# Mix loads, mix splits and first output weights of a streaming encoder step, moved among the sample pairs

## The chip, the cores and the metric

The kernel runs on one core of one Trainium2 chip. The metric is the device time of one execution in microseconds (us); lower is better. The engines are named as in the profile: PE (TensorE, matrix multiply; PEld is its weight load), DVE (VectorE), ACT (ScalarE), POOL (GpSimd) and SP (SyncE, which issues most of the DMA transfers, in program order).

## The reference

One layer of a streaming encoder, for a prompt of 1024 rows and a sample of 64 rows with caches. Cut to what matters here:

```python
h = rms_norm(xp, g_norm1[l])
qa, ka, va, qb, kb, vb, logf = in_proj(h, w_in[l], ...)
oa = chunk_band_attn_prompt(qa, ka, va, rel_bias[l])
ob = forget_attn_prompt(qb, kb, vb, logf)
xp = xp + jnp.concatenate([oa, ob], axis=-1) @ w_o[l]
mk, mv = mem_kv(mem_prompt, g_mem[l], w_mkv[l], g_mk[l])
...
oa = chunk_band_attn_sample(qa, ka, va, cache_a_k[l], cache_a_v[l], rel_bias[l])
ob = forget_attn_sample(qb, kb, vb, logf, cache_b_k[l], cache_b_v[l], cache_b_logf[l])
xs = xs + jnp.concatenate([oa, ob], axis=-1) @ w_o[l]
```

`concatenate([oa, ob])` is what the kernel calls the mix; the product with `w_o` is the output projection. The model width is 1024, the two attentions have 8 heads of 64 each, and the memory has 256 rows.

## The kernel before

Everything is computed in float32, each factor of a matmul split into a rounded high part and the rest as a low part: a product is three matmuls (high times high, low times high, high times low). A split is one cast on ACT (hi) and one subtraction on DVE or POOL (lo).

The stretch around the change lies between the prompt's attention, which ends at about 600 us, and the output projection, which begins at about 710 us. Three pieces of work share it.

**The memory's keys and values** (mem_piece, L679) are a list of pieces, `line`. Their weights come as loads `mwraw` of 512 KB (L661), two buffers, and are split in quarters, `mwhi` on ACT (L668) and `mwlo` on POOL or DVE (L669).

**The samples** are eight head pairs, one after the other (class Sample). For a pair, load fetches the query and key rows (`sqd`), the caches (`kraw`, `vraw`) and a bias; prep transposes and normalizes the query (`tq`, `sq`, `skn`); splitk and splitv split the caches (`kchi`, `kclo`, `vc`); score makes the scores `S` (L797, L798) and the exponential (L808); turn transposes the probabilities (`PT`, L822) and splits them (`pth` L823, `ptl` L824); sum multiplies them with the values into `O` (L835) and puts the halves together (`st` L842, `su` L843); out transposes `su` (L847) and copies it into `smix` (L849).

A loop over x = 0 to 8 weaves the steps of pair x, the rest of pair x - 1 and the preparation of pair x + 1 with `PER[x]` pieces of `line`. PER is (4, 8, 9, 12, 6, 5, 6, 0, 0), so at x = 7 `line` is empty.

**The prompt's mix** was written by the attention to a DRAM tensor `mixd`, eight tiles of 128 rows x 1024 columns. At x = 7, open_left closes the memory's buffers and, in their place, opens those of the weights (`wr`), of the first residual row (`x0`), of the split mix (`a`) and of four raw mixes (`mraw`). It loads the mixes (L976) and returns eight steps; each splits one tile over all 1024 columns, cast on ACT (L979) and subtraction on DVE (L980), and loads the mix four tiles on. The steps are woven in at x = 7. At x = 8 the first four weight tiles of `w_o` are split (class Stream: load L911, `hi` L919, `lo` L920) and the first product is woven in. After the loop the sample's columns are added to the split mix (L1022, L1023).

**The output projection** (project) goes over 8 tiles of output rows m and 3 chunks of columns c: 384, 384 and 320, the last with the sample's 64. A product of 24 matmuls (L937) fills a bank; DVE adds the residual row `qhi`, loaded by SP (L1066), in the evacuation (L1073), SP stores the result (L1074), and ACT, DVE and POOL make the operand and the square sum of the next norm (L1076 to L1083). ORDER starts with (m, c) = (0, 0), (0, 1), and these two products are the ones made early.

What stands in the code is not yet the order on the engines: a scheduler places the instructions of each engine.

Of the kernel before, what the change touches and what calls it, by code (L numbers as in the profile page):

```python
# [7 lines left out]
F32 = mybir.dt.float32  # L8
F32R = mybir.dt.float32r
ACT = mybir.ActivationFunctionType  # L10
ALU = mybir.AluOpType
# [4 lines left out]
P = 128  # L16
T = 1024
S = 64
N = T + S
D = 1024  # L20
KT = 8
# [6 lines left out]
PER = (4, 8, 9, 12, 6, 5, 6, 0, 0)  # L28
STAGE, MIXES = 4, 8
WARM = 20  # L30
# [4 lines left out]
CHUNKS = ((0, 384), (384, 384), (768, 320))  # L35
# [6 lines left out]
def hybrid_step(ctx: ExitStack, tc: tile.TileContext, i: dict, o: dict):  # L42
    nc = tc.nc
    act, dve, pool, pe = nc.scalar, nc.vector, nc.gpsimd, nc.tensor

    def f32(ap):
        return ap.bitcast(F32)
# [17 lines left out]
    mixd = dram.tile([8, P, T], F32, name="mixd")  # L65
# [38 lines left out]
    left = ExitStack()  # L104
# [355 lines left out]
    mixes = {}  # L460
# [183 lines left out]

    left = ExitStack()
    mp = left.enter_context(tc.tile_pool(name="mp", bufs=1, side="left"))
# [68 lines left out]
    class Sample:  # L715
# [180 lines left out]
    late_left, mixes = ExitStack(), ExitStack()  # L896
    stream = None

# [3 lines left out]
    class Stream:  # L902
# [52 lines left out]
    mixr = []  # L955
    first = [Product(2 * m, mixr, c, c == 2) for m, c in ((0, 0), (0, 1))]

# [4 lines left out]
    def open_left():  # L962
        nonlocal stream
        left.close()
        stream = Stream(late_left.enter_context(tc.tile_pool(name="wr", bufs=1, side="left")))
        x = late_left.enter_context(tc.tile_pool(name="x0", bufs=1, side="left")).tile([P, 384], F32, name="x0")
        nc.sync.dma_start(x, i["xT"][0, :, 0:384])
        ha = mixes.enter_context(tc.tile_pool(name="ha", bufs=1, side="left"))
        stage = rest.enter_context(tc.tile_pool(name="stage", bufs=1, side="left"))
        mixr.extend(parts(ha, "a"))  # L970
        stream.fetch()
        raws = {}

        def load_mix(k):
            raws[k] = stage.tile([P, T], F32, name="mraw", bufs=STAGE)
            nc.sync.dma_start(raws[k], mixd[k])  # L976

        def split_mix(k):
            act.copy(mixr[0][k][:, 0:T], raws[k])  # L979
            dve.tensor_tensor(mixr[1][k][:, 0:T], raws[k], f32(mixr[0][k][:, 0:T]), op=ALU.subtract)  # L980

        for k in range(STAGE):
            load_mix(k)

        def split_load(k):
            split_mix(k)
            if k + STAGE < KT:
                load_mix(k + STAGE)

        return ha, [lambda k=k: split_load(k) for k in range(KT)], x  # L990

    old, mixes_todo, ha = [], [], None
    todo = first[:]
    for x in range(len(samples) + 1):
        if not line and ha is None:
            ha, mixes_todo, early_x = open_left()
# [89 lines left out]

    ORDER = [(0, 0), (0, 1), (1, 0), (0, 2), (1, 1), (1, 2)] + [(m, c) for m in range(2, 8) for c in range(3)]

# [805 lines left out]
```

## Time and profile before

| | |
|---|---|
| median of 3 runs | 1781.4 us (1781.03 to 1784.44) |
| profiled execution | 1788.58 us, span 1786.6 us, granted clock 0.988 |
| busy share of the span | PE 96%, PEld 93%, DVE 68%, ACT 53%, POOL 36% |
| DMA | 199.87 MB, mean 112 GB/s |
| loads of a mix | 8 of 512 KB, median 5.0 us to landing |
| loads of memory weights | 16 of 512 KB, median 6.1 us to landing |

How to read the lines below. A row of the timeline has the start in us, the duration in us, the engine, the line in the kernel, the operation, output and inputs, shapes and a count; in brackets the idle time of the engine just before it, and what ended it. A row of the windows has a stretch, its length, and the busy time of each engine in it with the count of its instructions, then the granted clock of PE (1.00 is full speed), the busy share of the DMA engines and GB/s. A row of a line's instructions has the line, the engine, the operation and count, and the least, median and greatest duration in ns.

### The profile page before, as it was taken

Reading aid. Unit: us, or ns where it says so; the run is one execution under the profiler, and the core shown is the slowest. Engines: PE = TensorE matmul, PEld = TensorE weight load, DVE = VectorE, ACT = ScalarE, POOL = GpSimd, SP = SyncE. Lnnn points to the kernel's source line nnn. Section 1 sums busy time; section 2 is a strip of 40 time slices with the busy share of each in tenths; the row PEclk is TensorE's granted clock in tenths of the full one; section 3 lists DMA queues with packets and bytes.
Section 4 is the critical chain, followed back from the end, with each engine's and each line's share of the span. In section 5 each row is a group of like instructions: output and inputs, shape, how many; then the busy total and the mean of one; then the engine's idle time right before and its main releaser. Section 6 shows DMA issues by size and latency. Waiting matters only on the chain.

```text
span 1786.6 us, 33930 instructions
## 1 busy us (share of the span) xinstructions
PE 1717.5 (96%) x12432; PEld 1668.3 (93%) x12432; DVE 1210.5 (68%) x2643; ACT 941.2 (53%) x2058; POOL 647.3 (36%) x931
## 2 busy tenths in 40 slices
PE   7898999999998898999999999999999999999999
PEld 6888999999997777999999999999999999999999
DVE  5768667677677686433444369877777777649986
ACT  6756667677677577433555456434333333434432
POOL 4556667778777443453443612100000000000000
PEclk8999999999999999999999999999999999999999
DMA  7322222122112777541111563222222222693332
GB/s 251 91 62 64 60 77 78 49 74 76 51 56 83 216 252 219 165 143 56 54 54 60 151 214 104 79 75 77 79 85 85 85 73 73 216 346 130 118 104 88
DMA packets 134391, 199.87 MB, mean 112 GB/s; under 512 B 20984, under 2 KB 74360, under 8 KB 134224
## 3 DMA queue, kind: packets, MB, share of 16 engines
q1 hardware_dynamic: 134224, 197.70, 35.0%
q8 instruction: 98, 1.61, 0.4%
q14 instruction: 69, 0.57, 0.1%
HBM read 155.35 MB, written 45.44 MB: 112 GB/s over the span
## 4 chain that ended last, share of the span: by engine, by line
PE 46%; DVE 4%; issue 2%; ACT 1%; POOL 1%; DMA 1%; SPq 0%; DVEq 0%; ACTq 0%; POOLq 0%
PE W L1449 24%; PE W L1773 11%; PE pj L937 7%; PE S L1192 1%; PE tq L1228 1%; PE O L1228 1%; POOL lo L920 1%; DVE f L1314 0%; PE PT L1215 0%; DMA f<-x2d 0%; DVE lo L920 0%; DMA h<-ad 0%; PE O L1192 0%; ACT hi L1313 0%; DVE qhi L1301 0%
## 5 line engine op out<-in xcount | busy, mean ns | idle before, releaser
L299 PE MATMUL pj<-whi,xhi 128*128 128x384 f32 (+1 forms) x512 | 195.8, 382 | 2.7 <-DVE flog L314 1.6
L299 PE MATMUL pj<-wlo,xhi 128*128 128x384 f32 (+1 forms) x512 | 177.0, 346 | 4.3 <-POOL wlo L123 4.3
L299 PE MATMUL pj<-whi,xlo 128*128 128x384 f32 (+1 forms) x512 | 175.9, 344 | 0.7 <-DVE xlo L131 0.7
L1555 POOL COPY s<-gp 128x2 f32<-128x2 f32 x22 | 15.8, 720 | 335.8 <-DVE gp L1554 335.8
L1449 PE MATMUL W<-h,hi 128*128 128x272 f32 x704 | 134.4, 288 | 1.4 <-ACT qlo L1585 1.4
L504 ACT ACTIVATE s<-s,mx 128x640 f32<-128x640 f32 (+7 forms) x128 | 94.4, 737 | 77.4 <-DVE mx L502 76.5
L1773 PE MATMUL W<-f,hi 128*128 128x272 f32 x672 | 127.1, 287 | 0.1
L541 DVE TENSOR_TENSOR ptl<-PT,pth 128x512 fp32r<-128x512 f32 (+2 forms) x192 | 99.4, 522 | 37.5 <-ACT pth L540 35.3
L1449 PEld LDWEIGHTS W<-h,hi 128*128 128x128 f32 x704 | 110.8, 188 | 1.6 <-ACT qlo L1585 1.6
L540 ACT CAST pth<-PT 128x512 fp32r<-128x512 f32 (+2 forms) x192 | 84.7, 449 | 41.7 <-PE PT L539 39.9
L1773 PEld LDWEIGHTS W<-f,hi 128*128 128x128 f32 x672 | 105.3, 188 | 0.4 <-DVE f L1520 0.4
L299 PEld LDWEIGHTS pj<-wlo,xhi 128*128 128x128 f32 x512 | 99.5, 194 | 5.9 <-POOL wlo L123 5.9
L299 PEld LDWEIGHTS pj<-whi,xhi 128*128 128x128 f32 x512 | 99.4, 194 | 4.3 <-DVE flog L314 1.9
L1449 PE MATMUL W<-h,lo 128*128 128x272 f32 x352 | 101.8, 289 | 0.0
L299 PEld LDWEIGHTS pj<-whi,xlo 128*128 128x128 f32 x512 | 98.3, 192 | 1.4 <-DVE xlo L131 1.2
L1773 PE MATMUL W<-f,lo 128*128 128x272 f32 x336 | 96.7, 288 | 0.0
L539 PE MATMUL PT<-ident,s 128*128 128x128 f32 x528 | 89.9, 277 | 6.9 <-DVE ptl L541 5.4
L1313 ACT CAST hi<-raw 128x512 fp32r<-128x512 f32 x68 | 42.2, 621 | 98.6 <-PE W L1449 59.2
L499 PE MATMUL S<-kh,q 128*128 128x256 f32 (+1 forms) x304 | 77.8, 281 | 13.5 <-DVE mx L502 13.5
L937 PE MATMUL pj<-a,hi 128*128 128x384 f32 (+1 forms) x352 | 89.3, 337 | 0.2 <-DMA mraw<-mixd 0.2
L507 POOL TENSOR_SCALAR s<-s,ssum 128x640 f32<-128x640 f32 (+6 forms) x96 | 70.8, 738 | 47.9 <-DVE ssum L505 34.3
L554 PE MATMUL O<-pth,v 128*128 128x256 f32 (+1 forms) x304 | 76.5, 277 | 8.5 <-DVE mix L564 7.7
(538 smaller groups left out, 6037.6 us busy)
## 6 DMA issues: line engine op xcount, KB each, us to landing
raw<-in_w_down_dram SPq DMA_DIRECT2D x45, 256.0 KB, 2.8
wraw<-in_w_dram SPq DMA_DIRECT2D x56, 192.0 KB, 2.5
raw<-in_w_up_dram SPq DMA_DIRECT2D x41, 256.0 KB, 2.8
h<-ad SPq DMA_DIRECT2D x32, 272.0 KB, 5.5
mwraw<-in_w_mkv_dram SPq DMA_DIRECT2D x16, 512.0 KB, 6.1
raw<-in_w_mo_dram SPq DMA_DIRECT2D x32, 256.0 KB, 3.2
kvraw<-in_w_down_dram SPq DMA_DIRECT2D x32, 256.0 KB, 3.0
ad<-t SPq DMA_DIRECT2D x22, 272.0 KB, 2.2
```

The source lines that it names most:

```text
L299: pe.matmul(pj[:, :nw], x2[a][:, k, t * P:(t + 1) * P], wt[k][b][:, :nw], start=n == 0, stop=n == 3 * KT - 1)
L499: pe.matmul(sp[:, a:a + (k1 - k0) * P], q, kk[:, h, src], start=m == 0, stop=m == 1)
L504: act.activation(s[:, :n], s[:, :n], ACT.Exp, bias=mx, scale=-1.0, accum_out=sm)
L507: pool.tensor_scalar(s[:, :n], s[:, :n], sm, 1.0, op0=ALU.mult, op1=ALU.mult)
L539: pe.transpose(pt[:, b - ch[0]], self.s[j][:, (b - w0) * P:(b - w0 + 1) * P], ident)
L540: act.copy(hi[:, f:f + n, j], pt[:, f:f + n])
L541: dve.tensor_tensor(lo[:, f:f + n, j], pt[:, f:f + n], f32(hi[:, f:f + n, j]), op=ALU.subtract)
L554: pe.matmul(op[:, cols], groups[p, b // 2].v[:, b % 2, h].rearrange("p a d -> p (a d)"), pt[:, x, cols], start=b == self.full[0] and m == ...
L937: pe.matmul(out()[:, :cn], w[a][:, k % 4], x[b][k][:, c0:c0 + cn], start=k == 0 and n == 0, stop=k == KT - 1 and n == 2)
L1313: act.copy(hi, t)
L1449: pe.matmul(w[:, z, :Q], a(p, j), rights[j][b][:, z * Q:z * Q + Q], start=fresh and begin and j == 0 and x == 0, stop=final and end and j ...
L1773: pe.matmul(ws[m][:, z, :Q], la[p][:, m * P:(m + 1) * P], ra[b][:, z * Q:z * Q + Q], start=first and y == 0 and what in opening, stop=fina ...
```

## The change

The buffers of the weights and of the first residual row are opened before the memory's, so that they exist throughout. The mixes are loaded within the loop, at x = 4, 5 and 6 with two each and the last two in open_left, into five buffers of the samples' pool and three of the caches' `kraw` buffers. The query buffer `sqd` has one copy instead of two. Weights and residual row are fetched at x = 4, and the first four weight tiles are split at x = 5 and 6. The mix is split in two ranges of columns, 0 to 383 for all tiles and then 384 to 1023, sixteen steps instead of eight, eight of them at each x; the first product is woven with the second range. The second early product is (1, 0) instead of (0, 1), and ORDER follows.

```diff
-STAGE, MIXES = 4, 8
+MIXES = 8
+MIXED = {4: ("mraw",) * 2, 5: ("mraw",) * 2, 6: ("mraw", "kraw")}
+WEIGHTS = 5
...
-    left = ExitStack()
+    left, late_left = ExitStack(), ExitStack()
+    wr = late_left.enter_context(tc.tile_pool(name="wr", bufs=1, side="left"))
+    early_x = late_left.enter_context(tc.tile_pool(name="x0", bufs=1, side="left")).tile([P, 384], F32, name="x0")
     mp = left.enter_context(tc.tile_pool(name="mp", bufs=1, side="left"))
...
-            self.qd = mq.tile([S, 4, P], F32, name="sqd", bufs=2)
+            self.qd = mq.tile([S, 4, P], F32, name="sqd", bufs=1)
...
+    mraws = []
+
+    def load_mix(tag="mraw"):
+        k = len(mraws)
+        mraws.append(mq.tile([P, T], F32, name=tag, bufs={"mraw": 5, "kraw": 3}[tag]))
+        nc.sync.dma_start(mraws[k], mixd[k])
...
+    stream = Stream(wr)
...
-    first = [Product(2 * m, mixr, c, c == 2) for m, c in ((0, 0), (0, 1))]
+    first = [Product(2 * m, mixr, c, c == 2) for m, c in ((0, 0), (1, 0))]
...
     def open_left():
...
         left.close()
...
         mixr.extend(parts(ha, "a"))
...
-        def split_mix(k):
-            act.copy(mixr[0][k][:, 0:T], raws[k])
-            dve.tensor_tensor(mixr[1][k][:, 0:T], raws[k], f32(mixr[0][k][:, 0:T]), op=ALU.subtract)
...
-        return ha, [lambda k=k: split_load(k) for k in range(KT)], x
+        first_, rest_ = CHUNKS[0][1], slice(CHUNKS[0][1], T)
+
+        def split_mix(k, c):
+            hi, lo = (mixr[z][k][:, c] for z in range(2))
+            act.copy(hi, mraws[k][:, c])
+            dve.tensor_tensor(lo, mraws[k][:, c], f32(hi), op=ALU.subtract)
+
+        for k in range(6, KT):
+            load_mix("kraw")
+
+        return ha, [lambda k=k, c=c: split_mix(k, c) for c in (slice(0, first_), rest_) for k in range(KT)]
...
         if nxt:
             nxt.load()
+        for tag in MIXED.get(x, ()):
+            load_mix(tag)
+        if x == WEIGHTS - 1:
+            stream.fetch()
+            nc.sync.dma_start(early_x, i["xT"][0, :, 0:384])
...
-        if ha and not mixes_todo:
-            stream.upto(4)
-            if todo:
-                main = todo.pop(0).pieces
+        if WEIGHTS <= x < WEIGHTS + 2:
+            subs += [lambda n=n: stream.upto(n) for n in (2 * (x - WEIGHTS) + 1, 2 * (x - WEIGHTS) + 2)]
+        if ha and len(mixes_todo) <= KT:
+            main = todo.pop(0).pieces
         subs += mixes_todo[:MIXES]
...
-    ORDER = [(0, 0), (0, 1), (1, 0), (0, 2), (1, 1), (1, 2)] + [(m, c) for m in range(2, 8) for c in range(3)]
+    ORDER = [(0, 0), (1, 0), (0, 1), (0, 2), (1, 1), (1, 2)] + [(m, c) for m in range(2, 8) for c in range(3)]
```

Where this moves instructions shows in the order of the engines at three places. (Line numbers of the changed kernel are 2 to 12 higher.)

The first is ACT at the end of the prompt's attention, about 590 to 597 us in the profile before; `pth` are the casts of its probabilities, `s` its softmax. Before:

```order
L504 ACTIVATE s,ssum<-s,mx 128x896
L540 CAST pth<-PT 128x4x128
L540 CAST pth<-PT 128x3x128
L504 ACTIVATE s,ssum<-s,mx 128x1024
L509 ACTIVATE s<-s,ssum 128x896
L540 CAST pth<-PT 128x4x128 x2
L563 COPY otmp<-O 64x256
```

and with the change:

```order
L506 ACTIVATE s,ssum<-s,mx 128x896
L542 CAST pth<-PT 128x4x128
L929 CAST hi<-raw 128x512
L542 CAST pth<-PT 128x3x128
L506 ACTIVATE s,ssum<-s,mx 128x1024
L511 ACTIVATE s<-s,ssum 128x896
L542 CAST pth<-PT 128x4x128
L929 CAST hi<-raw 128x512
L542 CAST pth<-PT 128x4x128
L929 CAST hi<-raw 128x512
L565 COPY otmp<-O 64x256
```

Three casts of `w_o` weights (`hi<-raw`) have moved in between the last probability casts; in before, the first of them stands behind the last sample's transposes.

The second is SP at the loads of the last sample pair but one and of the last memory weights, about 676 us before:

```order
L740 DMA kraw<-in_cak_dram 128x512 x2
L744 DMA vraw<-in_cav_dram 128x512
L661 DMA mwraw<-in_w_mkv_dram 128x1024 x2
L702 DMA out_mv_dram<-kv 128x256
L703 DMA vmd<-kv 128x256
```

and with the change:

```order
L744 DMA kraw<-in_cak_dram 128x512 x2
L748 DMA vraw<-in_cav_dram 128x512
L902 DMA mraw<-mixd 128x1024 x2
L665 DMA mwraw<-in_w_mkv_dram 128x1024 x2
L706 DMA out_mv_dram<-kv 128x256
L707 DMA vmd<-kv 128x256
```

Two mixes now stand ahead of the two loads of memory weights.

The third is PE at the end of the samples, about 704 to 711 us before; `S` are the last pair's scores, `O` the weighted sums, `PT` the transposes of its probabilities, `pj<-a` the first product:

```order
L797 MATMUL S<-kclo,sq_9095 128x512
L835 MATMUL O<-vc,pth 128x256
L835 MATMUL O<-vc,ptl 128x256
L835 MATMUL O<-svh,pth 128x256
L835 MATMUL O<-svh,ptl 128x256
L847 MATMUL PT<-ident,su 64x128
L822 MATMUL PT<-ident,s 128x128 x4
L822 MATMUL PT<-ident,s 64x128
L937 MATMUL pj<-a_10467,hi 128x384
L937 MATMUL pj<-a_10475,hi 128x384
```

and with the change, at the start of the products:

```order
L839 MATMUL O<-vc,pth 128x256
L839 MATMUL O<-vc,ptl 128x256
L839 MATMUL O<-svh,pth 128x256
L839 MATMUL O<-svh,ptl 128x256
L949 MATMUL pj<-a_10506,hi 128x384 x2
L949 MATMUL pj<-a_10514,hi 128x384
L949 MATMUL pj<-a_10506,lo 128x384
L949 MATMUL pj<-a_10507,hi 128x384
```

Before, the first product starts behind the transposes of the last pair, and the last pair's sums stand within it; with the change all ten sums of the last pair stand ahead of the first product, and the two products (`x2` is one matmul of each) run side by side. In that order the query's transposes of the last pair (L758) and the sums of the pair ahead of it also stand behind the last memory matmul.

More of the change, by code (lines that the diff above doesn't have):

```diff
@@ L895, in hybrid_step @@
     step(0, [samples[0].prep, lambda: samples[0].splitk(0), lambda: samples[0].splitk(1)])
-    late_left, mixes = ExitStack(), ExitStack()
-    stream = None
+    mixes = ExitStack()
     srcs = [i[n][m][:, 4 * c:4 * c + 4] for n, ms in (("w_o", range(8)), ("w_mq", range(8)), ("w_mo", ROWS), ("w_mo", ROWS)) for m in ms for c in range(2)]
@@ L962, in open_left @@
     def open_left():
-        nonlocal stream
         left.close()
-        stream = Stream(late_left.enter_context(tc.tile_pool(name="wr", bufs=1, side="left")))
-        x = late_left.enter_context(tc.tile_pool(name="x0", bufs=1, side="left")).tile([P, 384], F32, name="x0")
-        nc.sync.dma_start(x, i["xT"][0, :, 0:384])
         ha = mixes.enter_context(tc.tile_pool(name="ha", bufs=1, side="left"))
-        stage = rest.enter_context(tc.tile_pool(name="stage", bufs=1, side="left"))
         mixr.extend(parts(ha, "a"))
[L971 to L976, printed above, removed]
-        def split_mix(k):
[L979 to L988, printed above, removed]
-        return ha, [lambda k=k: split_load(k) for k in range(KT)], x
+        first_, rest_ = CHUNKS[0][1], slice(CHUNKS[0][1], T)
[6 more added lines that the diff above has]
+        return ha, [lambda k=k, c=c: split_mix(k, c) for c in (slice(0, first_), rest_) for k in range(KT)]
     old, mixes_todo, ha = [], [], None
@@ L995, in hybrid_step @@
         if not line and ha is None:
-            ha, mixes_todo, early_x = open_left()
+            ha, mixes_todo = open_left()
         cur = samples[x] if x < len(samples) else None
```

## The prediction

> **What bounds the kernel now.** I read the page first, for the engine that is the bound.
>
> ```profile
> PE 1717.5 (96%) x12432; PEld 1668.3 (93%) x12432; DVE 1210.5 (68%) x2643; ACT 941.2 (53%) x2058; POOL 647.3 (36%) x931
> PE W L1449 24%; PE W L1773 11%; PE pj L937 7%; PE S L1192 1%; PE tq L1228 1%; PE O L1228 1%; POOL lo L920 1%; DVE f L1314 0%; PE PT L1215 0%; DMA f<-x2d 0%; DVE lo L920 0%; DMA h<-ad 0%; PE O L1192 0%; ACT hi L1313 0%; DVE qhi L1301 0%
> ```
>
> TensorE (PE) is busy 96% of the span and carries the chain of waits. The change leaves its matmuls as they are, so it can save only time in which PE idles, or in which it runs at a reduced clock. Next I cut the stretch of the change into windows.
>
> ```profile
> 680.00:700.00 20.00, 19.01 (x132) 16.18 (x131) 12.92 (x36) 13.84 (x36) 6.60 (x7) 1.00 0.67 211
> 700.00:710.00 10.00, 5.81 (x30) 4.18 (x30) 7.76 (x17) 8.90 (x20) 1.45 (x1) 0.85 0.75 232
> 710.00:725.00 15.00, 14.12 (x63) 12.62 (x63) 10.22 (x20) 9.07 (x23) 7.15 (x4) 0.76 0.53 174
> 725.00:740.00 15.00, 15.00 (x95) 15.00 (x94) 4.82 (x9) 6.07 (x12) 6.40 (x5) 1.00 0.68 206
> 760.00:806.00 46.00, 46.00 (x280) 46.00 (x279) 16.09 (x25) 16.76 (x32) 22.76 (x21) 1.00 0.45 144
> ```
>
> After each length come the busy times of PE, weight load, VectorE (DVE), ScalarE (ACT) and GpSimd (POOL), then granted clock, DMA share and GB/s. From 680 to 700 PE idles 1.0 us, from 700 to 710 4.2 us, from 725 on not at all. So the prize is what lies between 700 and 725: 5.1 us of idling (4.19 and 0.88) and a clock of 0.76 to 0.85. The timeline of that stretch says why.
>
> ```profile
> 703.68 0.40 PE L797 MATMUL S<-kclo,sq 128*128 128x512 f32 x1
> 705.05 0.78 ACT L808 ACTIVATE s<-s,mx 128x576 f32<-128x576 f32 x1 [0.95 <-DVE mx L807]
> 706.02 1.03 ACT L979 CAST a<-mraw 128x1024 fp32r<-128x1024 f32 x1
> 707.08 0.31 ACT L842 ACTIVATE st<-O,ssum 64x64 f32<-64x64 f32 x1
> 707.09 1.23 DVE L980 TENSOR_TENSOR a<-mraw,a 128x1024 fp32r<-128x1024 f32 x1 [0.48 <-ACT a L979]
> 708.34 0.29 DVE L843 SCALAR_TENSOR_TENSOR su<-O,ssum,st 64x64 f32<-64x64 f32 x1
> 708.78 0.39 PE L847 MATMUL PT<-ident,su 128*64 128x128 f32 x1 [4.03 <-DVE su L843]
> 709.02 1.31 PE L822 MATMUL PT<-ident,s 128*128 128x128 f32 x5
> 710.55 1.01 PE L937 MATMUL pj<-a,hi 128*128 128x384 f32 x2 [0.22 <-DMA mraw<-mixd]
> 724.76 0.51 PE L937 MATMUL PT<-a,hi 128*128 128x384 f32 x2
> ```
>
> The exponential of the last sample pair is done at about 706.0, yet PE stands still until 708.78: the two halves of su, which its next instruction reads, stand on ACT and DVE between whole 1024-wide splits of the mix (1.03 and 1.23 us). The first two products then run from 710.55 to 724.76. The last view is the granted clock, in windows of 3.41 us on the grid on which it changes in this trace.
>
> ```profile
> 17.57:20.99 3.42, 1.84 (x11) 1.52 (x10) 2.57 (x10) 3.42 (x12) 0.00 (x0) 1.00 0.93 277
> 92.67:96.08 3.41, 1.59 (x11) 1.30 (x11) 3.31 (x10) 1.31 (x4) 1.27 (x3) 1.00 0.24 53
> 703.65:707.06 3.41, 1.10 (x7) 0.72 (x5) 2.41 (x7) 2.45 (x5) 1.03 (x1) 1.00 0.82 255
> 707.06:710.48 3.42, 1.55 (x6) 0.97 (x6) 3.33 (x4) 3.32 (x7) 0.00 (x0) 0.50 0.88 271
> 713.89:717.30 3.41, 3.41 (x12) 3.41 (x12) 3.38 (x4) 2.72 (x10) 1.74 (x1) 0.50 0.88 326
> ```
>
> A window in which PE is busy 32% (703.65) is followed by half clock, and so is one of 47% (92.67); one of 54% (17.57) is not. The half clock lasts from 707.06 until after a full window, at 717.30. So in this trace about half a window of idling is enough to lose the clock.
>
> **The change, part by part.** The sum is made against the profiled execution, 1788.58 us (span 1786.6 us); the median of the runs is 1781.4 us, 7.18 us less, and the same difference is taken over to it.
>
> *Early weights.* Four splits of w_o weights go from behind 709 us into the end of the prompt's attention, three of them, by the order, before its last output.
>
> ```profile
> 590.00:606.00 16.00, 13.46 (x101) 11.93 (x101) 8.21 (x17) 8.88 (x19) 7.36 (x12) 1.00 0.70 189
> 596.64 0.38 PE L554 MATMUL O<-pth,v 128*128 128x256 f32 x1 [0.35 <-ACT pth L540]
> L919 ACT CAST hi<-raw x64: 602/620/635, 709.9 to 1073.0; 128x512 fp32r<-128x512 f32 x64
> L920 POOL TENSOR_TENSOR lo<-raw,hi x48: 1275/1293/2278, 710.6 to 1023.4; 128x512 fp32r<-128x512 f32 x48
> ```
>
> There PE waits for ACT's probability casts (0.35 us at 596.64), and the new casts of 0.62 us stand in front of such casts. If all three delay it: 3 x 0.62 = +1.9 us; if they fall into ACT's idle 45% (8.88 of 16 busy): 0. POOL is 46% busy there and takes its 1.29 us beside. I take +0.5, nearer the free end, since ACT is more often free than PE is waiting for it.
>
> *Mix loads beside the samples.* The mixes are 8 loads of 512 KB as before. Two of them now stand on the sync queue ahead of the last two loads of memory weights.
>
> ```profile
> 680.00:684.00 4.00, 4.00 (x30) 3.60 (x30) 2.79 (x7) 3.37 (x10) 1.66 (x2) 1.00 0.97 339
> 683.78 0.62 ACT L668 CAST mwhi<-mwraw 128x512 fp32r<-128x512 f32 x1 [0.43 <-DMA mwraw<-in_w_mkv_dram]
> 688.60 0.39 PE L679 MATMUL pj<-mwlo,mhi 128*128 128x256 f32 x1 [0.49 <-POOL mwlo L669]
> ```
>
> Here the DMA engines are full (0.97, 339 GB/s), and the weights arrive just in time: ACT waits 0.43 us for them at 683.78, PE 0.49 us for their split at 688.60. Two mixes ahead delay them by up to 2 x 524,288 bytes / 339 GB/s = 3.1 us. Behind them wait ACT's and POOL's splits, and PE behind those; its cover is the work of the sample pairs that the scheduler now places there. Between 0 and +3.1 I take +0.5, the row nearest to it, PE's present wait of 0.49, once more. That the query buffer has one copy instead of two costs at most one late small load, beside a full PE: 0.
>
> *The end of the samples.* The memory matmuls come earlier in PE's order, and behind the last of them stand only the two last sample pairs, one step after the other; both products come behind all of it. I walk this chain with durations of before.
>
> ```profile
> 698.44 0.40 PE L754 MATMUL tq<-ident,sqd 64*128 64x64 f32 x4
> 699.47 0.28 PE L679 MATMUL pj<-mwhi,mlo 128*128 128x256 f32 x1
> 700.31 0.87 PE L822 MATMUL PT<-ident,s 128*128 128x128 f32 x5
> 700.56 0.35 DVE L266 SCALAR_TENSOR_TENSOR skn<-tq,gd,skn 128x128 fp32r<-128x128 f32 x1 [0.63 <-ACT skn L265]
> 701.37 0.58 ACT L823 CAST pth<-PT 128x512 fp32r<-128x512 f32 x1
> 702.25 0.69 DVE L824 TENSOR_TENSOR ptl<-PT,pth 128x512 fp32r<-128x512 f32 x1
> 703.21 0.28 PE L835 MATMUL O<-vc,pth 128*128 128x256 f32 x1
> 703.33 0.28 PE L835 MATMUL O<-vc,ptl 128*128 128x256 f32 x1
> ```
>
> The last memory matmul ends at 699.75. To the end of the scores (704.08) it took 4.3 us, and 1.9 us more to the end of the exponential (705.05 + 0.97, with its accumulator read). Then come the transposes 0.87, the two halves of the probabilities 0.58 and 0.69, and ten sums at a step of 0.12 (703.21 to 703.33) = 1.2: together 9.6 us. But in before the query's transposes had been issued at 698.44, ahead of that end, and the sums of the pair ahead ran between the scores. In the new order both stand in the chain: from those transposes to the finished operand 700.91 - 698.44 = 2.5 us, and ten sums 1.2 us. So 13.3 us, and the products begin at 713.0 (710.55 before). The stall of 4.03 us goes, but a row of waits of a microsecond or two takes its place.
>
> Each product is 24 matmuls. At full clock one of 384 columns takes 46.00 / 280 = 0.164 us x 384 / 362.7 (mean width of chunks of 384, 384 and 320) = 0.174 us, two products 8.35 us. With full clock they end at 721.4, that is 3.4 us earlier than 724.76. But between 703.7 and 710.5 the chain gives PE some 3 us of work in 6.8 (transposes, ten sums, scores), so by the clock rows PE falls to half again near 707. Transposes and sums then cost 1.3 us more (1.31 for 0.87 in the row at 709.02, and the sums about 0.9 more), the products begin at 714.3, do 1.5 us of their work by 717.3, and end at 717.3 + 6.85 = 724.15: -0.6 us. If the clock comes back one window later, at 720.7, they end at 725.9: +1.1. I take -0.6.
>
> The Trainium skill, page "TensorE: Matmul & The Clock Gate", Part 1, "What's actually happening", says that the clock falls to half after at least one idle window of about 3.4 us. By that sentence no window of the new chain would cost the clock. The window of 3.41 us and the half rate agree with this trace; the idle window does not, since 703.65 to 707.06 held 1.10 us of work and half clock followed.
>
> *Splits in two ranges.* Eight 1024-wide splits become eight of 384 and eight of 640: per row the same elements, and eight more fixed starts on ACT and DVE. Both engines are free for 7.0 of the 25 us from 700 to 725 (8.90 + 9.07 busy on ACT, 7.76 + 10.22 on DVE), and the split of a 384-range is about 3/8 of 1.23 us, under the 0.52 us that three matmuls take. I take 0; without that cover it is eight starts of 2 x 0.62 - 1.03 = 0.2 us (two ACT casts of 512 columns against one of 1024), +1.6.
>
> *What comes behind.* A gain before 725 must pass the evacuations of the products.
>
> ```profile
> 724.24 0.56 DVE L1073 TENSOR_TENSOR qhi<-pj,x 128x384 f32<-128x384 f32 x1
> 739.48 0.56 DVE L1073 TENSOR_TENSOR qhi<-pj,qhi 128x384 f32<-128x384 f32 x1 [0.80 <-DMA qhi<-in_xT_dram]
> 740.21 0.56 PE L937 MATMUL pj<-a,hi 128*128 128x384 f32 x2
> ```
>
> At 739.48 the fifth evacuation waits 0.80 us for its residual row, and PE starts the product that takes over a bank at 740.21, 0.17 us after that evacuation ends. If that load on the sync queue comes no earlier, a gain stops there. I keep half of the -0.6: -0.3 us. The second product from the next row of the output needs the weights of two more tiles, which are there early now: 0.
>
> Sum: +0.5 + 0.5 - 0.3 = +0.7 us, so 1789.3 us profiled and 1782.1 us in the median.
>
> **The rivals.**
> 1. *The change does what its edit offers*: the chain is short, the stall of 4.03 us goes and no clock is lost. For it: su no longer waits behind 1024-wide pieces. Price: 4.03 + half of 6.75 us at half clock (710.55 to 717.30) = 7.4, less 1.0 of early costs: -6.4, 1775.0 us. Against it: the order puts two chains in series, and the evacuations would have to follow. Chance 0.17.
> 2. *The clock is kept* (waits of 1 to 2 us, none empties half a window): products end at 721.4; -3.4 + 1.0 = -2.4, 1779.0 us. For it: 54% busy kept the clock. Against it: the waits for exponential and casts come close together. The page named above would have this one. Chance 0.25.
> 3. *Slower, by the memory weights*: the two mixes ahead cost their full 3.1 us. A clock window that loses more than 1.8 us (53% of 3.41) has half clock behind it, 1.7 us more. Instead of +0.5 that is +4.8, so +5.0, 1786.4 us. It decides once the weights land later than the sums placed ahead of them last (1.2 us); the rows at 683.78 and 688.60 speak for it, the moved work against it. Chance 0.24.
>
> **How the numbers follow.** The forecast, waits and half clock in place of one stall, has 0.34. A measurement of this kernel can tell about 0.2%, 3.6 us, from no change. The first rival is faster than that, and I count a third of the second (0.08): 0.25. Slower is the third with 0.02 of the forecast: 0.26. The rest, 0.49, is within. The range leaves out half of the first rival's cases below 1775 and a third of the third's above 1787.5 (early casts in full, another +1.4 on top): 1775.0 to 1787.5.
>
> **What would show it.** In the changed kernel: no single wait of PE over 2.5 us between 695 and 715, but several of 0.5 to 2; a half-clock stretch that ends near 717; the first product near 714, the third at 724 to 725; PE's wait for the memory weights' splits near 685 to 690 under 1 us; the three new casts among the last probability casts near 590 to 597 with at most 0.5 us more idling on PE. The prediction is wrong if the products begin before 711, if the clock stays at 1.00, or if PE waits over 2 us near 686.

## The result, and the profile after

The changed kernel is slower. Its median is 1793.11 us (1791.70 to 1794.75, 4 runs) against 1782.04 us before: ratio 1.0058, interval 1.0043 to 1.0072. In a second set, on another occasion, the ratio was 1.0036 (1.0023 to 1.0050). So the loss is 4 to 13 us, about 6.5 in the one set and 11 in the other; forecast was +0.7. The profiled execution took 1792.5 us, span 1790.7 us.

The page and the windows, in the form shown for before:

```profile
PE 1718.0 (96%) x12432; PEld 1668.7 (93%) x12432; DVE 1211.6 (68%) x2651; ACT 942.1 (53%) x2066; POOL 642.3 (36%) x931
```

```profile
590.00:606.00 16.00, 13.86 (x100) 13.22 (x100) 7.52 (x16) 8.67 (x19) 10.99 (x16) 0.89 0.68 180
680.00:700.00 20.00, 17.98 (x128) 15.36 (x126) 12.33 (x32) 13.03 (x36) 5.72 (x5) 1.00 0.95 287
700.00:710.00 10.00, 5.78 (x23) 3.74 (x23) 4.68 (x14) 4.11 (x13) 1.79 (x2) 0.69 0.75 275
710.00:725.00 15.00, 13.54 (x63) 12.31 (x64) 10.09 (x20) 10.78 (x24) 0.00 (x0) 0.75 0.09 34
725.00:740.00 15.00, 15.00 (x95) 15.00 (x94) 7.15 (x20) 6.76 (x19) 6.10 (x5) 1.00 0.57 165
740.00:760.00 20.00, 17.39 (x96) 17.16 (x95) 7.38 (x12) 8.11 (x16) 10.31 (x9) 0.91 0.47 146
```

PE does the same work (1718.0 us busy against 1717.5). From 680 to 700 the DMA engines are now 95% busy instead of 67%, and PE idles 2.0 us instead of 1.0; from 700 to 710 PE is as idle as before, and ACT, 89% busy before, only 41%: the wait is no longer one behind splits. From 740 to 760, where before PE is busy throughout, it loses 2.6 us, and the clock falls. The timeline of the end of the samples, ahead of it two rows of before, its window from 740 to 760 and the exponential of the last pair but one:

```profile
740.00:760.00 20.00, 20.00 (x120) 19.95 (x119) 7.35 (x12) 8.04 (x16) 10.27 (x10) 1.00 0.48 148
697.43 0.78 ACT L808 ACTIVATE s<-s,mx 128x576 f32<-128x576 f32 x1 [1.42 <-DVE mx L807]
```

```profile
697.84 0.77 ACT L812 ACTIVATE s<-s,mx 128x576 f32<-128x576 f32 x1 [0.83 <-DVE mx L811]
698.76 0.76 PE L826 MATMUL PT<-ident,s 128*128 128x128 f32 x5 [0.73 <-ACT s L812]
701.90 0.46 PE L758 MATMUL tq<-ident,sqd 64*128 64x64 f32 x4
704.09 1.04 PE L802 MATMUL tq<-skn,sq 128*128 128x64 f32 x4 [1.44 <-DVE skn L268]
705.39 0.42 ACT L853 COPY smix<-PT 64x64 f32<-64x64 f32 x2 [1.50 <-PE PT L851]
705.84 1.14 ACT L778 CAST kchi<-kraw 128x512 fp32r<-128x512 f32 x2
706.51 0.80 PE L801 MATMUL S<-kchi,sq 128*128 128x512 f32 x1 [1.15 <-ACT kchi L778]
708.25 0.63 PE L801 MATMUL S<-kclo,sq 128*128 128x512 f32 x1
709.85 0.78 ACT L812 ACTIVATE s<-s,mx 128x576 f32<-128x576 f32 x1 [2.35 <-DVE mx L811]
710.77 1.33 PE L826 MATMUL PT<-ident,s 128*128 128x128 f32 x5 [1.89 <-ACT s L812]
715.86 0.69 PE L949 MATMUL pj<-a,hi 128*128 128x384 f32 x1
721.54 0.42 ACT L853 COPY smix<-PT 64x64 f32<-64x64 f32 x2 [2.11 <-PE PT L851]
724.22 2.29 DVE L983 TENSOR_TENSOR a<-kraw,a 128x640 fp32r<-128x640 f32 x3
725.20 0.51 PE L949 MATMUL PT<-a,hi 128*128 128x384 f32 x2
726.43 1.16 DVE L1026 TENSOR_TENSOR a<-smix,a 128x64 fp32r<-128x64 f32 x8
727.80 0.56 DVE L1076 TENSOR_TENSOR qhi<-pj,x 128x384 f32<-128x384 f32 x1
729.40 0.45 PE L949 MATMUL PT<-a,hi 128*128 128x320 f32 x2
743.41 0.59 PE L949 MATMUL pj<-a,hi 128*128 128x384 f32 x2 [2.61 <-DVE qhi L1076]
```

The two exponentials (697.84 and 709.85) are those of the last two pairs. They lie 12.0 us apart; before it was 7.6 us (697.43 and 705.05). Between them PE meets waits of 0.73, 1.44 and 1.15 us in a chain that before ran among other work. The reader should look at 705.39: ACT stands idle 1.50 us for the transposes of the pair ahead, and only then casts the last pair's keys. Their loads had been issued at 695.3 and 695.7 and landed in 4.6 to 4.8 us, so the keys lay ready about 5 us earlier. This part is a matter of order, not of late data.

What follows is a second loss. In this pair of profiles the third product starts at 725.20, only 0.4 us later than before (724.76), so most of the 4.4 us has been made up by then. But the first evacuation, which before began at 724.24, half a microsecond ahead of the third product, begins at 727.80, 2.6 us behind it. On DVE it stands behind the last splits of the mix (724.22) and the sample's columns (726.43); these come late because ACT, ahead of its last five casts, stood idle 2.11 us for the transposes of the last pair (721.54). The seventh product then waits 2.61 us for an evacuation to free its bank (743.41).

The table gives, for the profiles of all kernels, the lengths between fixed events, worked out from the starts in their timelines: (A) last copy of the attention's output on ACT to the first copy of a memory value; (B) from there to the exponential of the last pair but one; (C) to that of the last pair; (D) from there to the fourth product, the first of 320 columns (728.97 before, 729.40 with the change); (E) from there to the 24th evacuation.

| kernel | A | B | C | D | E | sum |
|---|---|---|---|---|---|---|
| before (profile of the prediction) | 56.1 | 40.8 | 7.6 | 23.9 | 86.1 | 214.6 |
| before, second profile | 55.0 | 40.7 | 7.6 | 23.1 | 86.1 | 212.5 |
| before + second row | 54.5 | 41.2 | 7.6 | 23.9 | 86.1 | 213.3 |
| before + weights early | 54.8 | 40.4 | 9.2 | 20.2 | **87.9** | 212.4 |
| before + buffers early | 54.7 | 41.1 | 7.6 | 20.4 | **90.7** | 214.6 |
| before + pieces | 54.2 | 40.8 | 7.6 | 24.0 | 86.1 | 212.6 |
| before + pieces and second row | 54.2 | 40.7 | 7.6 | 24.1 | 86.1 | 212.7 |
| before + mix loads alone | 53.5 | 41.6 | **13.1** | 28.2 | 86.1 | 222.5 |
| before + mix loads, behind the last pair | 52.9 | 40.9 | 7.6 | **35.2** | 86.1 | 222.7 |
| changed | 55.8 | 42.3 | **12.0** | 19.5 | **90.5** | 220.1 |
| changed, second profile | 54.0 | 42.1 | **12.0** | 20.9 | **90.1** | 219.1 |
| changed, weights late | 56.9 | 41.5 | **11.5** | 19.6 | **90.4** | 219.9 |
| changed, second tile of the same row | 59.1 | 42.1 | **12.0** | 19.6 | **90.6** | 223.4 |
| changed, mixes one step later | 57.8 | 40.8 | **11.7** | 23.4 | **88.0** | 221.6 |
| changed, whole splits | 57.8 | 42.1 | **12.0** | 19.5 | **90.5** | 221.9 |
| changed, mixes behind the last pair | 55.4 | 40.6 | 8.8 | 24.2 | **88.9** | 217.9 |
| the same, weights late | 55.7 | 40.5 | 7.6 | 25.2 | **87.5** | 216.6 |
| changed, mixes on ACT's queue | **62.3** | 39.1 | 8.0 | 21.8 | **89.9** | 221.1 |
| changed, mixes on POOL's queue | **63.0** | 40.4 | 8.6 | 16.9 | **90.1** | 219.1 |

The sums of the seven profiles without mix loads beside the samples are 212.4 to 214.6 us, those of all others 216.6 to 223.4.

Column E splits the kernels sharply. It is 86.1 us in the seven profiles in which the buffers of the weights are opened late, as before, with mix loads beside the samples or without. It is 87.5 to 90.7 in the twelve in which they are opened early, each time with a wait of PE of 1.2 to 2.7 us for an evacuation ahead of the seventh product. Column C is long, 11.5 to 13.1, where mixes stand on SP ahead of the last pair's loads.

### The profile page after: what moved, and what is told of

Its sections match the earlier page's. It is cut to its first block, busy times and chain, and to the rows that moved or that the text cites. A ratio compares the mean times of both kernels' runs of the same rounds, so it can differ in the third digit from the quotient of the medians.

```text
span 1790.7 us, 33940 instructions
## 1 busy us (share of the span) xinstructions
PE 1718.0 (96%) x12432; PEld 1668.7 (93%) x12432; DVE 1211.6 (68%) x2651; ACT 942.1 (53%) x2066; POOL 642.3 (36%) x931
## 4 chain that ended last, share of the span: by engine, by line
PE 48%; DVE 3%; issue 1%; ACT 1%; POOL 1%; DMA 0%; SPq 0%; ACTq 0%; DVEq 0%; POOLq 0%
PE W L1452 25%; PE W L1776 11%; PE pj L949 7%; PE W L949 1%; PE S L1195 1%; PE tq L1231 1%; PE O L1231 1%; POOL lo L930 1%; PE PT L1218 0%; DVE f L1317 0%; DMA f<-x2d 0%; PE O L1195 0%; ACT hi L1316 0%; PE PT L1176 0%; POOL s L1210 0%
## 5 line engine op out<-in xcount | busy, mean ns | idle before, releaser
L542 ACT CAST pth<-PT 128x512 fp32r<-128x512 f32 (+2 forms) x192 | 84.6, 448 | 42.3 <-PE PT L541 40.6
```

The costliest lines, as they stand in the source:

```text
L542: act.copy(hi[:, f:f + n, j], pt[:, f:f + n])
```

## The experiments

The first question was whether the profile of before, 7 us above its median, holds something unusual.

> The kernel before once more, to see whether its profiled execution of 1788.6 us (7 us above its median) holds a stretch that its other runs do not have. Theory: the difference between the kernels in the profile from 542 to 830 us is +7.3 us, and in the medians +11.1 us, so a usual execution of the kernel before has about 4 us less of waiting or half clock somewhere. If the second profile is near 1781 us, the place where it is shorter is that place. Rival: the profiles of the kernel before are all near 1788 us, and the profiler adds the difference.

Measured: 1783.3 us, span 1781.3 us. Its columns A and D are together 1.9 us shorter than in the first profile; the granted clock is 0.992 instead of 0.988. The first profile had more half clock, not another order, so the rows that the prediction rests on stand, but the distance between the two profiles of record (4.1 us of span) is smaller than that of the medians.

**One part of the change undone.** Weights late:

```diff
-        if WEIGHTS <= x < WEIGHTS + 2:
-            subs += [lambda n=n: stream.upto(n) for n in (2 * (x - WEIGHTS) + 1, 2 * (x - WEIGHTS) + 2)]
         if ha and len(mixes_todo) <= KT:
+            stream.upto(4)
             main = todo.pop(0).pieces
```

> The changed kernel with the first four weight tiles split where they were before, at the first product, and no longer among the last probability casts of the attention. Theory A (the three casts stand in front of probability casts, +1.8 us in the profile from 588 to 601 us): 1791.3 us, and the offset of the memory's first unit against the kernel before stays at about -2.5 us instead of -0.7. Theory B (the early casts are hidden, the +1.8 us is the clock or chance): unchanged, 1793.1 us. Splits behind the samples may cost up to 1 us there.

Measured: 1.0032 (1.0021 to 1.0044). Fetch and first residual row were moved to open_left as well. This lies under both ratios of the change but within their spread. The run does not test what was expected of it. The buffers are still opened early, and its trace shows that the scheduler put the three casts among the last probability casts all the same, where the changed kernel has them (587.86, 592.23 and 593.69):

```profile
586.88 0.62 ACT L929 CAST hi<-raw 128x512 fp32r<-128x512 f32 x1
591.26 0.62 ACT L929 CAST hi<-raw 128x512 fp32r<-128x512 f32 x1
592.74 0.63 ACT L929 CAST hi<-raw 128x512 fp32r<-128x512 f32 x1
```

What moved are later weight loads on SP: three at 707.21 instead of one at 690.16 and two at 701.52.

Second tile of the same row:

```diff
-    first = [... for m, c in ((0, 0), (1, 0))]
+    first = [... for m, c in ((0, 0), (0, 1))]
```

> The changed kernel with the second early product taken from the same row and the next columns, as before. Theory A (with the second tile from the next row, the weights' third split waits and the seventh product stands still 2.6 us at 743.4 us, and a window of half clock follows, 1.7 us): 1789 us, PE without idling from 725 to 805 us. Theory B (the seventh product waits for the fifth evacuation, which its residual load sets whatever the order): unchanged at 1793.1 us.

Measured: 1.0052 (1.0032 to 1.0071); PE waits 2.72 us for the evacuation before the seventh product, as before the edit (2.61). Theory A falls: the row is not what makes it wait.

Mixes one step later, so that the memory weights stand ahead of them:

```diff
-MIXED = {4: ("mraw",) * 2, 5: ("mraw",) * 2, 6: ("mraw", "kraw")}
+MIXED = {5: ("mraw",) * 2, 6: ("mraw",) * 3 + ("kraw",)}
```

> The changed kernel with no mix loaded at x = 4: two at x = 5 and four at x = 6, so that the last two loads of memory weights stand ahead of all mixes. Theory A (the mixes ahead delay those weights, +1.5 us at the end of the memory matmuls): the memory's last unit comes 1.5 us earlier, 1791.6 us. Theory B (the end of the samples is set by the last pair's own chain, not by the memory matmuls): the last unit comes earlier, but the first product does not, 1793.1 us.

Measured: 1.0041 (1.0026 to 1.0055). Column B falls from 42.3 to 40.8: the delay by the two mixes ahead of the memory weights, 1.5 us, is real and goes. Column C stays at 11.7, since two mixes still stand ahead of the last pair's loads. The first product starts no earlier: theory B.

Whole splits of 1024 columns, the product behind all of them:

> The changed kernel with each mix tile split whole again, 1024 columns at once, and the first product behind all splits. Theory A (the two ranges are free and help the first product to start early): +1 to +3 us on the changed kernel, 1.0070 times the kernel before. Theory B (the start of the products is set by the last pair's chain): the same as the changed kernel, 1.0055.

Measured: 1.0042 (1.0032 to 1.0053). The two ranges neither gain nor cost.

**One part of the change alone**, on the kernel before. The mix loads, with the buffers they need:

```diff
-STAGE, MIXES = 4, 8
+MIXED = {4: ("mraw",) * 2, 5: ("mraw",) * 2, 6: ("mraw", "kraw")}
...
+        for tag in MIXED.get(x, ()):
+            load_mix(tag)
```

> The kernel before with one part of the change alone: the eight mixes are loaded beside the sample pairs, into the same buffers as in the change (which takes the second copy of the query buffer), while weights, whole-tile splits and the second product stay as before. In its order the pair sums and scores of the last two pairs already stand one behind the other ahead of the products, two value splits stand ahead of the memory weights' split on POOL in the third step, and two mixes ahead of the last memory weights. Theory A (this part carries most of the loss): 1.7 us near 630, 1.5 us near 690 and 4.4 us at the last pair's exponential, together +7.6 us, 1.0043 times the kernel before. Theory B (the loss is in the early weights and the second tile): within 1.0010.

Measured: 1.0033 (1.0020 to 1.0046), +5.8 us in the medians. This part alone loses as much as the change did in its second set, but only in part at the same places. Column C is 13.1, as long as in the change. Here the weights' loads, late as before, queue behind the mixes too, and PE waits 4.94 us for their split, a wait that the change does not have; and column E, long in the change, is untouched.

```profile
703.88 0.78 ACT L809 ACTIVATE s<-s,mx 128x576 f32<-128x576 f32 x1 [2.02 <-DVE mx L808]
714.90 1.01 PE L945 MATMUL pj<-a,hi 128*128 128x384 f32 x2 [4.94 <-ACT hi L927]
```

Buffers of weights and residual row opened early, nothing else:

> The kernel before with the buffers of the weights and of the first residual row opened ahead of the memory's, as in the change, and nothing else. The scheduler then moves the weights' loads and three of their splits into the end of the attention by itself, and the first product ahead of the transposes of the last pair. Theory A (three casts of 0.62 us in front of probability casts cost about 1 to 1.8 us, and the products gain less than that at the other end): +0.5 to +1.8 us. Theory B (the products fill the wait of 4 us at the end of the samples): -2 to -5 us, 0.998.

Measured: 1.0001 (0.9992 to 1.0011). The products do start earlier (703.3 us, ahead of the last exponential), column D is about 3 us shorter, and column E 4.6 us longer: the seventh product waits 2.58 us for an evacuation. What is gained ahead of the evacuations is lost in them. So early buffers alone bring the loss of column E.

Second row alone:

> The kernel before with only the second early product from the next row of the output, (1, 0) for (0, 1). The order of PE up to there is the same. Theory A (the third and fourth weight tiles' turn-over and the evacuations of two rows then leave PE waiting before the seventh product, 2.6 us and a half-clock window of 1.7 us): +2 to +4 us. Theory B (the wait before the seventh product in the changed kernel comes from the late evacuation, not from the row): within 1 us of the kernel before.

Measured: 0.9995 (0.9986 to 1.0005), no difference.

Weights early alone, pieces alone (each tile in 384 and 640 columns, one behind the other, as the loads of before allow), and pieces with the second row:

> The kernel before with the early weights of the change alone: buffers opened early, loads at x = 4, splits at x = 5 and 6; mixes as before. Theory A (the early weights cost 1 to 2 us at the end of the attention and give it back at the first product, whose low part waited 0.66 us for a weight split): within 0.0010 of the kernel before. Theory B (they carry the 1 to 3 us by which the changed kernel with late weights was faster): 1.0010 to 1.0017.

> The kernel before, with loads as before, and each mix tile split in two pieces of 384 and 640 columns one behind the other. Theory A (PE's wait of 4 us for the last pair but one comes from whole splits of 1.0 and 1.2 us ahead of su on ACT and DVE): the wait falls by about 1 us, the first product starts 1 us earlier, 0.9990 to 1.0000. Theory B (the order of su among the splits sets it, not their size; the evacuations cap what is gained): no change, within 0.0005.

> Pieces and second row together, the two parts of the change that showed no loss or were not tried alone, with loads and weights as before. If both help a little (second row 0.9995, pieces 0.9995), this is the version that beats both kernels: 0.9990. If the evacuations cap the gain: 0.9995 to 1.0005.

Measured: 1.0006 (0.9997 to 1.0015), 1.0003 (0.9994 to 1.0012) and 1.0009 (1.0000 to 1.0017). None of them carries the loss, and pieces and second row together beat nothing. (The first expectation's bounds do not separate its two theories at 1.0006; with 1.0015 as the upper end, at most 2.7 us are theirs.)

**Where the loads stand.** The next three ran beside the changed kernel on one chip:

> The changed kernel once more, beside the next three on the same chip, so that they can be compared with it: 1.0045 to 1.0070 times the kernel before.

Measured: 1.0036 (1.0023 to 1.0050). Six mixes behind the last pair's loads:

```diff
-MIXED = {4: ("mraw",) * 2, 5: ("mraw",) * 2, 6: ("mraw", "kraw")}
+MIXED = {6: ("mraw",) * 5 + ("kraw",)}
```

> The changed kernel with six of the eight mixes loaded at x = 6, behind the loads of the last sample pair, and none at x = 4 and 5; the rest of the change stays. In its order the query's transposes of the last pair stand ahead of the last memory matmuls again, and its scores between the sums of the pair ahead, as before the change; the products stay behind the last pair's sums. Theory A (the mixes ahead of the last pair's loads make the scheduler put the two last pairs in series, +4.4 us, and delay the last memory weights, +1.5 us): 1.001 to 1.002 times the kernel before, 5 to 6 us under the changed kernel, the last exponential within 1 us of the end of the memory as in the kernel before. Theory B (what costs is the products' place behind the last pair's sums, and half clock, whatever the mixes do): as the changed kernel, 1.005.

> The same with the weights split at the first product, as before the change. Theory A: the early weights' share, 1 to 3 us, goes too: 1.000 times the kernel before, within 0.0015. Theory B: 1.003, as with the weights late alone.

> The kernel before with the mix loads alone, six of them behind the loads of the last pair instead of ahead. Theory A (the place ahead of the last pair's loads is what costs): 1.000, where the loads ahead gave 1.0033. Theory B (that the mixes are loaded beside the samples at all, the shared buffers and the traffic, is what costs): 1.003.

Measured: 1.0021 (1.0012 to 1.0030), 1.0012 (1.0003 to 1.0022) and 1.0036 (1.0023 to 1.0049). In all three the last pairs run interleaved again: column C is 8.8, 7.6 and 7.6. In the first two 0.0015 and 0.0024 of the 0.0036 of that set go with it; the interval of the first overlaps that of the change, that of the second ends just below it. The second does not show the share of the early splits either, since its casts stand early too (588.68, 592.11 and 593.11). The third shows theory A to be too narrow: C is whole, but the weights' loads now stand behind 4 MB of mixes, PE waits 8.72 us for their split, and column D is 35.2. In the first, the mixes themselves land late:

```profile
703.04 0.77 ACT L812 ACTIVATE s<-s,mx 128x576 f32<-128x576 f32 x1
712.02 1.28 PE L949 MATMUL pj<-a,hi 128*128 128x384 f32 x2 [1.05 <-ACT a L982]
740.22 0.59 PE L949 MATMUL pj<-a,hi 128*128 128x384 f32 x2 [1.59 <-DVE qhi L1076]
```

The products start 9.0 us behind the last exponential (5.5 before), and the wait before the seventh product stays at 1.59 us, here with evacuations that wait for their residual rows (3.08 and 2.21 us).

Last, the loads at their place in the program but on another engine's queue:

```diff
-        nc.sync.dma_start(mraws[k], mixd[k])
+        nc.scalar.dma_start(mraws[k], mixd[k])   # or nc.gpsimd
```

> The changed kernel with the eight mix loads issued by ACT instead of SP; nothing else is changed, the loads stay at x = 4 to 7. In its order the last memory weights and the last pairs' loads have no mix ahead of them on SP, the last pair's scores stand ahead of the sums of the pair before, and the products start ahead of the last pair's transposes. Theory A (the place in SP's queue, and the order that the scheduler makes of it, is what costs): 1.000 or under, the products' start at the last exponential. Theory B (the traffic of 4 MB beside the samples costs, whatever queue it is on): 1.0035 to 1.005. Issuing eight loads may cost ACT 0.4 us each.

> The same with the loads issued by POOL, which is less busy there (29% against 69% for ACT from 680 to 700 us in the changed kernel). Its order has the interleaved end of the samples too. Theory A: 1.000 or under. Theory B: 1.0035 to 1.005.

Measured: 1.0045 (1.0032 to 1.0058) with ACT, 1.0018 (1.0009 to 1.0028) with POOL. Each theory is right about a part. Off SP's queue the last pairs are interleaved (C 8.0 and 8.6), and with POOL the products start with the last exponential, D 16.9, the shortest of all. But the scheduler now issues five mixes between 602 and 618 us (POOL), and column A is 6 to 8 us longer than before. (ACT is 65% busy from 680 to 700 us in the changed kernel; the 69% of the expectation are those of the kernel before.) Windows and timeline with POOL's queue:

```profile
600.00:610.00 10.00, 7.06 (x56) 6.51 (x56) 7.86 (x14) 4.35 (x14) 6.30 (x10) 1.00 0.67 208
610.00:620.00 10.00, 5.99 (x33) 5.69 (x33) 5.04 (x13) 3.90 (x12) 4.08 (x5) 0.72 0.97 324
```

```profile
614.95 0.66 PE L758 MATMUL tq<-ident,sqd 64*128 64x64 f32 x4 [4.01 <-DMA sqd<-sqk]
708.95 1.04 PE L949 MATMUL pj<-a,hi 128*128 128x384 f32 x3 [0.84 <-ACT a L982]
```

With the DMA engines 97% busy, PE waits 4.01 us for a sample's query of 128 KB, and the clock falls. The load was issued on SP at 607.03, 7.9 us ahead of its use; in the changed kernel the same load, behind the same loads of its queue, was issued at 607.97 and used without a wait 4.4 us later.

## Why the prediction was wrong

Two steps failed. The walk of the samples' end was too short; and, the larger one, the stretch behind the first products was counted only as a cap on a gain, with nothing for a loss.

- **What bounds the kernel**, and where: right. The loss lies in the waits and half clock of PE between the attention and the end of the output projection, columns A to E.
- **Early weights, +0.5**: the term holds for the place that it was for. The three casts stand between two copies of the attention's output on ACT. That stretch takes 8.3 us with them (586.67 to 594.95, second profile of the changed kernel) and 8.1 without (587.46 to 595.54, before); a window of half clock makes it 9.8, with the casts (the first profile of the changed kernel) and without (pieces and second row). Alone the early weights measure 1.0006 (0.9997 to 1.0015), +1.1 us with an interval across zero. What their buffers cost behind the products is told under the last point.
- **Memory weights behind two mixes, +0.5**: the mechanism is right, the size was off. Column B is about 1.5 us longer (42.3 and 42.1 against 40.8 and 40.7), and with the mixes behind those weights it is 40.8 again. The last two loads of memory weights land in 8.2 and 10.2 us, against 7.0 and 8.8 before: 1.2 and 1.4 us later, not 3.1. In the trace:

```profile
675.66 0.91 SPq L902 DMA_DIRECT2D mraw<-mixd  x2
676.67 1.21 SPq L665 DMA_DIRECT2D mwraw<-in_w_mkv_dram  x2
687.42 1.14 ACT L672 CAST mwhi<-mwraw 128x512 fp32r<-128x512 f32 x2 [0.35 <-DMA mwraw<-in_w_mkv_dram]
687.62 0.39 PE L683 MATMUL pj<-mwlo,mhi 128*128 128x256 f32 x1 [0.47 <-POOL mwlo L673]
```

  By itself this moved little: mended alone, the kernel stayed at 1.0041, because the products behind it began no earlier.
- **The end of the samples, -0.6 before its halving**: this walk failed. The prediction walked a chain of 13.3 us from the last memory matmul to the first product, 14.6 with half clock. It measures 18.0 us (697.85 to 715.86): 11.0 to the end of the scores (708.88), where the walk has 8.0, and 7.0 from there, where it has 6.6. The walk began with the transposes of the pair ahead as if its exponential were done. But the memory matmuls had been pulled so far ahead that this exponential ends only at 698.7, after the last of them; and ACT's casts of the last pair's keys stand behind the copies of the pair ahead, which the walk did not follow on ACT (it idles 1.50 us there, PE 0.73 ahead of it and 1.15 behind it). Column C is 4.4 us longer and D 3.3 us shorter, since the stall of 4.03 us is gone. With B, the memory to the fourth product takes 2.5 us more in the mean of the profiles (1.5 and 3.6), where +0.5 and -0.6 were forecast. That the third product starts at 725.20, near the forecast 724.15, is in part luck: the memory matmuls ended 1.9 us earlier than in the walk, and the chain behind them was 3.4 us longer.
- **Half clock near 707**: it came, and one window earlier than forecast, at 703.8. Its row and the one before it, on the grid of this execution, and ahead of them another window that half clock followed:

```profile
632.10:635.51 3.41, 2.17 (x14) 1.78 (x15) 2.47 (x6) 2.83 (x8) 2.55 (x3) 1.00 1.03 369
700.37:703.78 3.41, 2.00 (x14) 1.46 (x14) 1.59 (x6) 1.41 (x5) 0.46 (x1) 1.00 1.03 399
703.78:707.19 3.41, 1.95 (x6) 1.29 (x6) 1.39 (x6) 1.87 (x6) 0.00 (x0) 0.50 0.56 211
```

  PE was busy 59% of the window ahead of the drop. So the reading that about half a window of idling loses the clock holds as to the kind (no idle window is needed), but not as to the bound: 54% kept it in the trace of before, 59% lost it here, and so did the 64% near 632.
- **Splits in two ranges, 0**: right (alone 1.0003; taken back in the change 1.0042).
- **What comes behind, and the second row, 0**: this is the step that failed by most. The evacuations were named as a cap on a gain, and a loss in them was put at nothing. Column E is 86.1 us in both profiles of before and 90.5 and 90.1 in those of the change: +4.0 to +4.4 us. Of this, PE's wait before the seventh product is 2.61 and 2.39 us, and most of the rest is a window of half clock behind it (1.7 us). In the trace the first evacuation begins late because DVE still has the mix to split: the eight splits, which before were spread over the waits of the samples from 705 on, all come behind the last exponential. Buffers opened early, alone, bring the same column E (90.7), and mix loads alone do not (86.1). The row of the second tile has no part in it, nor have the two ranges.

Column by column, in the mean of the two profiles of each kernel, A is 0.7 us shorter, B 1.4 longer, C 4.4 longer, D 3.3 shorter and E 4.2 longer. That is about 6 us, where the medians differ by 6.6 and 11. The third rival, slower by the memory weights, had the right side with the wrong place.

The prediction did not weigh either where the mixes were loaded before: three of the eight within the attention's end, where the DMA engines are 63% busy (timeline and window of before):

```profile
578.92 1.38 SPq L976 DMA_DIRECT2D mraw<-mixd  x3
```

```profile
575.00:590.00 15.00, 8.50 (x48) 7.18 (x49) 13.32 (x23) 11.62 (x24) 12.03 (x14) 0.69 0.63 213
```

The change loads none before 675.7, and six of its eight pass the DMA engines while the samples' and the memory's loads need them. The kernels with loads pay for it wherever it is put: ahead of the last pairs in C, behind them in D where the weights come after them, on another queue in A. But before does not owe its time to the three early loads: the kernels with weights or buffers early load only one mix there (578.06 and 578.73) and the other seven from 698 and 700 on, behind all loads of the samples, and are as fast.

Not settled: what exactly holds the evacuations back in column E. In the changed kernel it is read from the trace, and no run moved the first evacuation by itself; with the mixes behind the last pair the first evacuation is early enough, and PE waits all the same. The ratio of the same changed kernel differed between two sets (1.0058 and 1.0036, intervals that overlap), and a window of half clock near 635 us stands in one of its two profiles. Why the scheduler puts the last pairs in series with mixes ahead was read from its order only: the seven profiles with mixes on SP ahead of the last pair's loads have C at 11.5 to 13.1, the other twelve at 7.6 to 9.2. No kernel was found that is faster than before.

## What to carry to other kernels

A load that is moved ahead must be charged for whose loads it now stands in front of, both on its queue and in the DMA engines: find in the trace the stretch where they are free, and ask whether the old place was already there. Where the move makes a scheduler reorder two chains from side by side to one behind the other, walk the chain on every engine that it crosses, from the first operation that isn't done, and not on the bound engine alone. And a gain ahead of a ring of banks is worth only what the ring lets through; work that a move pushes later on the evacuating engine can turn that gain into a loss. Last, look in the trace whether an edit moved what it was to move: here a scheduler put splits back where the edit had taken them from.

## What the runs showed of the hardware

- A load's own queue did not protect it: with the mixes on POOL's queue, a 128 KB load on SP's queue held PE up for 4.01 us while the DMA engines were 97% busy at 324 GB/s (7.9 us from issue to use, against 4.4 without those mixes).
- The clock fell to half after windows of 32% (before), 59% and 64% (changed) of busy PE, and was kept after one of 54% (before): the busy share in the profile alone doesn't tell when it falls. The window of 59% held 0.46 us of transposes (the row at 701.90).
- Two profiles of the same kernel differ by up to 5.3 us of span (1786.6 and 1781.3) with the same order, in part by windows of half clock: 0.988 and 0.992 mean granted clock.
